# Hybrid encoder layer: first head pair's bias and cached k and v loaded behind the first norm, FFN block order, one more low part by DMA

## Chip, cores, metric

One core of a Trainium2 chip runs the whole layer in one launch. The metric is the device time of one execution in microseconds. TensorE (PE) does the matrix products, ScalarE (ACT) activations and copies, VectorE (DVE) and GpSimd (POOL) elementwise work, SyncE (SP) issues most of the transfers; POOL issues those that add into a tile.

## The reference

One inference step of one encoder layer for 512 new prompt frames and 64 frames of a running stream, 576 tokens of width 1024:

```python
h = layer_norm(ALPHA * x + 0.5 * swiglu_ffn(x, w_gu1, w_down1), g1, b1)
z = h @ w_in     # mLSTM q,k,v,o,i,f | attention q,k,v | two branch gates
# attention: 16 heads of 64, frames in chunks of 64, each sees its own and 8 chunks before;
# the stream's 64 frames see 256 cached k and v as well
s = einsum('bhqd,bhkd->bhqk', q, kk) + bias
o = einsum('bhqk,bhkd->bqhd', softmax(s), vv)
mix = (sigmoid(g_ml) * mlstm(...) @ w_ml + sigmoid(g_att) * o @ w_att) @ w_out
h = layer_norm(ALPHA * h + mix, g2, b2)
y = layer_norm(ALPHA * h + 0.5 * swiglu_ffn(h, w_gu2, w_down2), g3, b3)
```

with `swiglu_ffn(x) = (silu(gate) * up) @ w_down`, 2816 hidden columns. The outputs are `y`, the new mLSTM state, and the new k and v.

## The kernel before

**Products.** Every fp32 operand is split into a high part rounded to fp32r and a low part, the rest; a product is three matmuls, high by high, high by low and low by high (`mm`, L128). Weights come in blocks of 128x1024: SP loads `wr` (L208), ACT rounds it to `wh` (`act`, L142), and the low part `wl` comes in one of two ways. Either DVE subtracts (`tt`, L145). Or, for the keys in the set `ADDED`, ACT writes the negated high part into `wl` and POOL issues a second transfer of the same block that adds into it (`add_lo`, L180 to L182). `pump` (L193ff) keeps two raw and up to four split blocks ahead of the products.

**Units.** Most gate and up blocks of both FFNs, and 14 pairs of column blocks of `w_in`, go in units of seven products on sums and differences instead of eight products (`GateUp`, `Columns`). `Combos` makes the sums of the activations (`add`, DVE) and splits them (`make`, ACT, with the low part by POOL's adding DMA, into tiles `tx`, of which there are `NX`). `prep` splits a unit's weights: "a" (rows as loaded), "s" (sums into `ws` and `wt`), "t" and "u" (these sums), "b" (half a block, `ah` and `al`). `run` works through the units: first `begin` with the "a" part, then sums s2, s1, s3.

**Stages.** FFN 1 from 0 to about 395 us, the first norm and the first blocks of `w_in` (v, k, q of the first attention pair, and the mLSTM gates) to 440, column units to 520, attention with its eight pairs of heads to 790, gates and projections, the mLSTM, the output product with the second norm from 1160 to 1204, FFN 2 to the end with the last norm.

**Order.** PE's order is written out by the program: the class `Order` holds a heap of steps with due times (`later`) and takes them as the counted time of the matmuls passes. The other engines' orders come from a scheduler that follows PE's order, with priorities (`hot`, `high_priority`) and explicit successions (`issue_after`). Each engine then runs its list in order, so an instruction that waits holds up all behind it.

**Attention, per pair j of heads.** `att_qkv` (L1090ff) loads the bias `G` (two tiles of 128x512, `bias`, L1095 to L1105; POOL masks a corner of each, L1102), the cached values `vp` (L1111) and the cached keys `kp` (L1112). POOL splits `vp` into `vc` (L152 and L145), and `dup` splits keys into `kh` and `kl` for each head e of the pair and copies them to the other half of the partitions: for the new keys `kf` POOL and ACT write `kh`, DVE subtracts and copies `kl` (L1151); for the cached keys POOL does all. `att_core` computes `score(e, i)`, four blocks for each head, with softmax, transposes (`turn`) and split (`pth`, `ptl`), then `values(e)`; after the first head's scores comes `score_s`, the stream's 64 queries on cached and new keys. The due times of the steps count from the pair's start; the loads of pair 0 are issued there too, since the tiles of this stage's pool come free only at the end of the stage before.

Of the kernel before, what the change touches and what calls it, by code (L numbers as in the profile page):

```python
# [81 lines left out]
def tile_layer(ctx: ExitStack, tc: tile.TileContext, ins, outs):  # L82
# [71 lines left out]
    def pround(out, in_):  # L154
# [9 lines left out]
    NX = 10  # L164
# [4 lines left out]
        | {("ap", j) for j in range(KT)} | {("gu2", 1, 1), ("gu2", 2, 0)}  # L169
# [10 lines left out]
    def add_lo(lo, hi, src):  # L180
        act(lo, f(hi), scale=-1.0)
        POOL.dma_start(lo, src, accum_op=ALU.add)  # L182
# [10 lines left out]
    def pump(limit=2):  # L193
        while True:
# [16 lines left out]
            if c < wst["stop"] and c < wst["taken"] + limit and wst["used"] < NWB:  # L211
# [3 lines left out]
                if plan[c][0] == "if":  # L215

                    r3 = raw[:, :n].rearrange("p (k c) -> p k c", c=64)
                    h3 = hi.rearrange("p (k c) -> p k c", c=P)
                    act(h3[:, :, 0:64], r3)
                    tt(h3[:, :, 64:128], r3, f(h3[:, :, 0:64]), ALU.subtract)  # L220
                    parts[c] = (hi, None)
                else:
                    lo = wpool.tile([P, 1024], F32R, tag="wl", name=nm("wl"), bufs=NWB)
                    step = n if plan[c][0] not in PIECES else 512
                    for a in range(0, n, step):
                        act(hi[:, a:a + step], raw[:, a:a + step])
                        if plan[c][0] in ADDED:
                            add_lo(lo, hi, plan[c][1])
                            continue
                        before = wst.pop("behind", None)  # L230
                        with tc.issue_after(before.ins) if before is not None else nullcontext():
                            tt(lo[:, a:a + step], raw[:, a:a + step], f(hi[:, a:a + step]), ALU.subtract)
                    parts[c] = (hi, lo)
# [419 lines left out]
    class Combos:  # L653


        def __init__(self, xs, raw, sums):
            self.xs, self.raw, self.n, self.sums = xs, raw, 0, sums
            self.b = {}

        def tile(self):  # L660
            self.n += 1
            return slot(F32R, self.pool, "tx", bufs=NX) if self.n <= NX else slot(F32R)

# [10 lines left out]
        def make(self, middle):  # L674
# [3 lines left out]
            for n, (ka, kb) in ((1, ("t2", "t4")), (0, ("t1", "t3"))):  # L678
                for i in range(4):

                    t, hi, lo = self.sums[2 * i + n], self.tile(), self.tile()
                    with tc.issue_after(after.ins) if after is not None else nullcontext():
                        last = ACT.activation(hi, t, AF.Copy)
                        add_lo(lo, hi, t)
# [9 lines left out]
    class Units:  # L694
# [78 lines left out]
        def run(self, tail):  # L773
            cur = ahead = None
            for j in self.js + [None]:
# [13 lines left out]
                if j == self.js[0]:  # L789

# [107 lines left out]
    def ffn(xs, n, gi, raw, final=None, prev=None):  # L898
        hh = {}
        with tc.tile_pool(name=nm("hr"), bufs=FT, side="right", reuse_waits="tile") as hr, \  # L900
# [11 lines left out]
            def up_cb(j):  # L912
                return lambda hf, ps: tt(hs(hh[j], hf), hs(hh[j], hf), ps, ALU.mult)
# [29 lines left out]
            with wstack, tc.tile_pool(name=nm("st"), bufs=1, side="right", reuse_waits="tile") as un.tp, \  # L943
# [24 lines left out]
                after = un.prep(j0, "u")  # L968
                with tc.issue_after(after.ins):
                    un.prep(j0, "b")  # L970
# [120 lines left out]
    def att_qkv(j):  # L1091
        ap_ = apool[0]
        st = {}
        def bias():
            G = st["G"] = ap_.tile([P, 2, 512], F32, tag="G", name=nm("G"))  # L1095
# [3 lines left out]
            @hot(0 if j else 300)  # L1099
# [4 lines left out]
            later(4000 if j else 0, mask)  # L1104

        if j == 0:
            bias()
        vc = ap_.tile([P, 7, 2, P], F32R, tag="vc", name=nm("vc"), bufs=2)
        vp = ap_.tile([P, 2, P], F32, tag="vp", name=nm("vp"))
        kp = ap_.tile([P, NPAST], F32, tag="kp", name=nm("kp"))  # L1110
        SP.dma_start(vp, ins["vpast"][:, :, j * P:(j + 1) * P])  # L1111
        SP.dma_start(kp, ins["kpastT"][:, j, :])  # L1112
# [68 lines left out]
    def att_core(j, st):  # L1181
# [27 lines left out]
        def score(e, i):  # L1209
# [6 lines left out]
            ttr(sc[:, :w], ps[:, :w], G[:, e, 512 - w:512], mx[:, 0:1])  # L1216
# [26 lines left out]
        def score_s():  # L1243
            sc, mx = tiles()
            for e in range(2):
# [6 lines left out]
                ttr(sc[r, :320], ps[0:64, :320], G[0:64, e, 128:448], mx[r, 0:1])  # L1252
# [42 lines left out]
    combos = Combos(H, ln1.d, [slot(F32, stp, "st", bufs=8) for _ in range(8)])  # L1295
# [24 lines left out]
    ln1.close()  # L1320
    with tc.tile_pool(name="cx", bufs=1, side="right", reuse_waits="tile") as cx:
# [22 lines left out]
        after = un.prep(0, "u")  # L1344
        with tc.issue_after(after.ins):
            un.prep(0, "b")
# [479 lines left out]
```

## Time and profile before

| | |
|---|---|
| median of 3 runs | 1598.27 us (1597.28, 1598.27, 1598.95) |
| the profiled execution | 1598.74 us, its span 1597.0 us |
| PE busy | 1570.4 us, 98% |
| DVE, ACT, POOL busy | 1066.0, 885.2, 187.1 us |
| mean granted clock | 0.996 |
| moved by DMA | 202.88 MB, mean 127 GB/s |

A row of a timeline has its start, its duration, the engine, the line, the operation, output and inputs by the program's names, shape, and count; in brackets stands how long the engine had been idle before it and what ended that. A row with a count over 1 is a run of such instructions, and its duration is of them all together. A row of waits has the total, the number and the longest in microseconds. A window row has, for a stretch, each engine's busy time and instructions, then the granted TensorE clock, the DMA engines' share and the rate.

### The profile page before, as it was taken

The numbers are of one execution on the slowest core, as the hardware profiler recorded it, in microseconds if no ns is written. First come the engines' busy times: TensorE is split into PE (matmuls) and PEld (weight loads), VectorE is DVE, ScalarE is ACT, GpSimd is POOL, SyncE is SP. The second block draws the span as 40 slices with busy tenths as digits, with TensorE's granted clock in tenths as the row PEclk, the third lists the DMA queues.
The fourth block names the chain that finished last, engine by engine and source line by source line (L and its number), as shares of the span: only waits on it lengthen the run. The fifth ranks groups of instructions, "written<-read, shape, count | busy, mean of one in ns | idle before, by whom it ended". The sixth has DMA issues, their size and how long they took to land. (4 is left out here: it accounts for less than half of the span.)

```text
span 1597.0 us, 29481 instructions
## 1 busy us (share of the span) xinstructions
PE 1570.4 (98%) x11767; PEld 1548.2 (97%) x11767; DVE 1066.0 (67%) x2126; ACT 885.2 (55%) x1627; POOL 187.1 (12%) x350
## 2 busy tenths in 40 slices
PE   9999999999999899999999999999999999999998
PEld 8999999999999799999999999999999999999997
DVE  7777777627766657667613677755677787786636
ACT  7444455324855667777745876664456445454223
POOL 2000000000300433432111111101111000000000
PEclk9999999999999999999999999999999999999999
DMA  9232322225743666665788555543554222213333
GB/s 253 106 106 80 106 80 73 83 87 167 184 138 122 170 144 148 161 148 131 202 201 203 139 133 116 126 116 117 161 130 100 80 106 82 105 53 98 111 93 123
DMA packets 72113, 202.88 MB, mean 127 GB/s; under 512 B 7976, under 2 KB 17832, under 8 KB 71976
## 3 DMA queue, kind: packets, MB, share of 16 engines
q1 hardware_dynamic: 58584, 159.31, 30.7%
q0 software_dynamic: 12816, 41.16, 15.4%
q8 instruction: 92, 1.51, 0.4%
q10 hardware_dynamic: 576, 0.52, 0.1%
q14 instruction: 45, 0.37, 0.1%
HBM read 177.57 MB, written 16.32 MB: 121 GB/s over the span
## 5 line engine op out<-in xcount | busy, mean ns | idle before, releaser
L128 PE MATMUL mm<-s,wh 128*128 128x288 f32 (+2 forms) x3606 | 738.1, 298 | 1.5 <-ACT wh L142 0.9
L128 PEld LDWEIGHTS mm<-s,wh 128*128 128x128 f32 x3606 | 579.6, 189 | 5.5 <-ACT wh L142 1.1
L128 PE MATMUL mm<-s,wl 128*128 128x288 f32 (+2 forms) x1787 | 529.3, 296 | 1.1 <-DVE wl L145 1.1
L128 PEld LDWEIGHTS mm<-s,wl 128*128 128x128 f32 x1787 | 337.9, 189 | 1.7 <-DVE wl L145 1.7
L142 ACT ACTIVATE wh<-wr 128x1024 fp32r<-128x1024 f32 (+2 forms) x148 | 149.2, 1010 | 245.8 <-PE mm L128 225.3
L145 DVE TENSOR_TENSOR wl<-wr,wh 128x1024 fp32r<-128x1024 f32 (+2 forms) x87 | 100.1, 1155 | 101.1 <-ACT wh L142 101.1
L128 PE MATMUL mm<-h,wh 128*128 128x256 f32 (+1 forms) x672 | 134.7, 294 | 0.0
L128 PEld LDWEIGHTS mm<-h,wh 128*128 128x128 f32 x672 | 107.6, 188 | 0.2
L128 PE MATMUL mm<-tx,wh 128*128 128x288 f32 x522 | 107.0, 296 | 0.0
L128 PE MATMUL mm<-h,wl 128*128 128x256 f32 (+1 forms) x336 | 98.7, 294 | 0.0
L145 DVE TENSOR_TENSOR wl<-wt,wh 128x1024 fp32r<-128x1024 f32 x46 | 56.4, 1226 | 55.1 <-ACT wh L717 55.1
L717 ACT ACTIVATE wh<-wt 128x1024 fp32r<-128x1024 f32 x46 | 48.8, 1060 | 74.0 <-DVE wt L145 73.0
L450 POOL TENSOR_TENSOR rs<-var,mhalf 128x2 f32<-128x2 f32 (+1 forms) x6 | 5.2, 866 | 720.6 <-DVE var L148 720.6
L128 PEld LDWEIGHTS mm<-tx,wh 128*128 128x128 f32 x522 | 83.7, 188 | 0.0
L128 PE MATMUL mm<-tx,wl 128*128 128x288 f32 x261 | 77.0, 295 | 0.0
L182 POOL DMA_DIRECT2D wl<-in_w_in x50 | 44.0, 881 | 262.0 <-ACT wl L142 220.0
L128 PE MATMUL mm<-tx,ah 128*128 128x288 f32 x344 | 70.4, 297 | 0.0
L145 DVE TENSOR_TENSOR wl<-wu,wh 128x1024 fp32r<-128x1024 f32 x46 | 56.3, 1224 | 21.1 <-ACT wh L717 21.1
L142 ACT ACTIVATE h<-h 128x288 f32<-128x288 f32 x78 | 34.2, 438 | 63.8 <-DVE h L145 63.7
L717 ACT ACTIVATE wh<-wu 128x1024 fp32r<-128x1024 f32 x46 | 48.7, 1059 | 34.6 <-PE mm L128 33.9
L145 DVE TENSOR_TENSOR wl<-ws,wh 128x1024 fp32r<-128x1024 f32 x46 | 56.1, 1220 | 11.6 <-ACT wh L717 11.6
L142 ACT ACTIVATE wl<-wh 128x1024 fp32r<-128x1024 f32 x60 | 63.4, 1056 | 0.6
(342 smaller groups left out, 3485.0 us busy)
## 6 DMA issues: line engine op xcount, KB each, us to landing
wu<-in_w_gu SPq DMA_DIRECT2D x78, 512.0 KB, 4.4
wr<-in_w_in SPq DMA_DIRECT2D x58, 512.0 KB, 4.0
wl<-in_w_in POOLq DMA_DIRECT2D x50, 512.0 KB, 5.8
wr<-in_w_dn SPq DMA_DIRECT2D x40, 512.0 KB, 3.6
wr<-in_w_dn SPq DMA_DIRECT2D x20, 384.0 KB, 3.1
wu<-in_w_in SPq DMA_DIRECT2D x14, 512.0 KB, 4.8
G<-in_rbias SPq DMA_DIRECT2D x16, 256.0 KB, 2.9
wr<-in_w_ap SPq DMA_DIRECT2D x8, 512.0 KB, 4.7
```

The lines of the kernel that those rows point to most:

```text
L128: PE.matmul(out, lhsT, rhs, start=start, stop=stop, **kw)
L142: ACT.activation(out, in_, func, **kw)
L145: return (eng or DVE).tensor_tensor(out, a, b, op=op)
L182: POOL.dma_start(lo, src, accum_op=ALU.add)
L450: return y, POOL.tensor_tensor(y, v, mhalf[:, :n], op=ALU.pow)
L717: self.last = ACT.activation(hi, src, AF.Copy)
```

## The change

- **First attention pair.** The bias tiles, `vp` and `kp` of pair 0 are no longer loaded at the start of the attention stage. They go into tiles of the general slots (`past0`, `G0`), with the four loads written right behind the sums of the first norm, after `ln1.close()`; POOL's two masks follow the last adding DMA of `make` (`combos.added`). `G` becomes a list of two tiles. The other pairs' loads keep their text, and since pair 0 has none of its own there, the scheduler issues pair 1's earlier; in POOL's order the masks of pair 1 come to stand on either side of pair 0's last `kl` copy, where pair 0's own masks stood near the front.
- **tx tiles.** The units of `w_in` get 11 of them instead of 10 (`NX_IN`).
- **Second pair's first weight block sooner.** In the first round of `run`, for FFN 1, FFN 2 and the column units, "a" of the next unit is split ahead of "u" and "b" of the first; these two moved from before `run` into it.
- **FFN 1.** The multiplication by `up` of block 0 is set behind the low part of block (1,1) on DVE (`wst["lo"]`).
- **FFN 2.** The block (2,1) of gate and up joins `ADDED`: its low part by ACT's negated copy and POOL's adding DMA instead of DVE's subtraction.

PE's list of matmuls and their order are the same.

```diff
--- before.py
+++ after.py
@@ -161,12 +161,12 @@
     WARM = 8
     LAST = {1: 6, 2: 6}
     CL = {1: 2, 2: 3}
-    NX = 10
+    NX, NX_IN = 10, 11
     NH0, NH1 = 1, 6
     PIECES = {("in", 48), ("in", 40), ("in", 32)}
 
     ADDED = {("in", c + j) for c in (32, 40, 48) for j in range(2, KT)} | {("in", c) for c in (*range(32), *range(56, 72))} \
-        | {("ap", j) for j in range(KT)} | {("gu2", 1, 1), ("gu2", 2, 0)}
+        | {("ap", j) for j in range(KT)} | {("gu2", 1, 1), ("gu2", 2, 0), ("gu2", 2, 1)}
 
     EARLY = [("gu2", 0, 0), ("gu2", 0, 1), ("gu2", 1, 0)]
     EARLY1 = [("in", 16), ("in", 17)]
@@ -179,7 +179,7 @@
 
     def add_lo(lo, hi, src):
         act(lo, f(hi), scale=-1.0)
-        POOL.dma_start(lo, src, accum_op=ALU.add)
+        return POOL.dma_start(lo, src, accum_op=ALU.add)
 
     def early(pool, key, group):
         c = [k for k, _ in plan].index(key)
@@ -229,7 +229,7 @@
                             continue
                         before = wst.pop("behind", None)
                         with tc.issue_after(before.ins) if before is not None else nullcontext():
-                            tt(lo[:, a:a + step], raw[:, a:a + step], f(hi[:, a:a + step]), ALU.subtract)
+                            wst["lo"] = tt(lo[:, a:a + step], raw[:, a:a + step], f(hi[:, a:a + step]), ALU.subtract)
                     parts[c] = (hi, lo)
                 wst["used"] += 1
                 wst["conv"] += 1
@@ -653,13 +653,13 @@
     class Combos:
 
 
-        def __init__(self, xs, raw, sums):
-            self.xs, self.raw, self.n, self.sums = xs, raw, 0, sums
+        def __init__(self, xs, raw, sums, nx=NX):
+            self.xs, self.raw, self.n, self.sums, self.nx = xs, raw, 0, sums, nx
             self.b = {}
 
         def tile(self):
             self.n += 1
-            return slot(F32R, self.pool, "tx", bufs=NX) if self.n <= NX else slot(F32R)
+            return slot(F32R, self.pool, "tx", bufs=self.nx) if self.n <= self.nx else slot(F32R)
 
         def add(self, i):
             r1, r2 = self.raw[4 + i], self.raw[i]
@@ -681,7 +681,7 @@
                     t, hi, lo = self.sums[2 * i + n], self.tile(), self.tile()
                     with tc.issue_after(after.ins) if after is not None else nullcontext():
                         last = ACT.activation(hi, t, AF.Copy)
-                        add_lo(lo, hi, t)
+                        self.added = add_lo(lo, hi, t)
                     d = self.b.setdefault(i, {})
                     d[ka], d[kb] = (hi[:, a], lo[:, a]), (hi[:, b], lo[:, b])
                 if n:
@@ -787,6 +787,10 @@
                 with tc.high_priority(offset=90 if j == self.js[0] else 0):
                     self.prep(j + 1, "a")
                 if j == self.js[0]:
+                    with tc.issue_after(self.lo.ins):
+                        after = self.prep(j, "u")
+                    with tc.issue_after(after.ins):
+                        self.prep(j, "b")
 
                     ahead = self.begin(j + 1, "aux")
                 with tc.issue_after(self.lo.ins):
@@ -910,7 +914,10 @@
                 return cb
 
             def up_cb(j):
-                return lambda hf, ps: tt(hs(hh[j], hf), hs(hh[j], hf), ps, ALU.mult)
+                def cb(hf, ps):
+                    with tc.issue_after(wst["lo"].ins) if prev is None and j == 0 else nullcontext():
+                        tt(hs(hh[j], hf), hs(hh[j], hf), ps, ALU.mult)
+                return cb
 
             def key(j, e):
                 return [((f"gu{n}", j, e), KT)]
@@ -965,9 +972,6 @@
                         with tc.issue_after(combos.last.ins):
                             un.prep(j0, "s")
                         un.prep(j0, "t")
-                after = un.prep(j0, "u")
-                with tc.issue_after(after.ins):
-                    un.prep(j0, "b")
                 un.load(j0 + 2)
 
                 def tail():
@@ -1092,24 +1096,28 @@
         ap_ = apool[0]
         st = {}
         def bias():
-            G = st["G"] = ap_.tile([P, 2, 512], F32, tag="G", name=nm("G"))
+            G = ap_.tile([P, 2, 512], F32, tag="G", name=nm("G"))
+            st["G"] = [G[:, e, :] for e in range(2)]
             for e in range(2):
                 SP.dma_start(G[:, e, :], ins["rbias"][2 * j + e])
 
-            @hot(0 if j else 300)
             def mask():
                 for e in range(2):
                     POOL.memset(G[0:64, e, 448:512], NEG)
 
-            later(4000 if j else 0, mask)
-
+            later(4000, mask)
+
+        vc = ap_.tile([P, 7, 2, P], F32R, tag="vc", name=nm("vc"), bufs=2)
         if j == 0:
-            bias()
-        vc = ap_.tile([P, 7, 2, P], F32R, tag="vc", name=nm("vc"), bufs=2)
-        vp = ap_.tile([P, 2, P], F32, tag="vp", name=nm("vp"))
-        kp = ap_.tile([P, NPAST], F32, tag="kp", name=nm("kp"))
-        SP.dma_start(vp, ins["vpast"][:, :, j * P:(j + 1) * P])
-        SP.dma_start(kp, ins["kpastT"][:, j, :])
+            st["G"], vp, kp = G0, vp0, kp0
+            with tc.issue_after(combos.added.ins):
+                for e in range(2):
+                    POOL.memset(G0[e][0:64, 448:512], NEG)
+        else:
+            vp = ap_.tile([P, 2, P], F32, tag="vp", name=nm("vp"))
+            kp = ap_.tile([P, NPAST], F32, tag="kp", name=nm("kp"))
+            SP.dma_start(vp, ins["vpast"][:, :, j * P:(j + 1) * P])
+            SP.dma_start(kp, ins["kpastT"][:, j, :])
         vp4 = vp.rearrange("p b (e c) -> p b e c", c=64)
         for b in range(2):
             pround(vc[:, 5 + b, :, 0:64], vp4[:, b])
@@ -1213,7 +1221,7 @@
             mm(ps[:, :w], q, kh[:, e, :w], True, False)
             mm(ps[:, :w], q, kl[:, e, :w], False, True)
             sc, mx = tiles()
-            ttr(sc[:, :w], ps[:, :w], G[:, e, 512 - w:512], mx[:, 0:1])
+            ttr(sc[:, :w], ps[:, :w], G[e][:, 512 - w:512], mx[:, 0:1])
             softmax(sc, mx, w, lambda: turn(e, i, sc))
 
         def turn(e, i, sc):
@@ -1249,7 +1257,7 @@
                     mm(ps[0:64, s0:s0 + n], q, kh[:, e, kk:kk + n], True, False)
                     mm(ps[0:64, s0:s0 + n], q, kl[:, e, kk:kk + n], False, True)
                 r = slice(64 * e, 64 * e + 64)
-                ttr(sc[r, :320], ps[0:64, :320], G[0:64, e, 128:448], mx[r, 0:1])
+                ttr(sc[r, :320], ps[0:64, :320], G[e][0:64, 128:448], mx[r, 0:1])
             softmax(sc, mx, 320, lambda: turn_s(sc))
 
         def turn_s(sc):
@@ -1292,7 +1300,7 @@
     stp = pstack.enter_context(tc.tile_pool(name="st", bufs=1, side="right", reuse_waits="tile"))
     e1 = pstack.enter_context(tc.tile_pool(name="early1", bufs=1, side="right", reuse_waits="tile"))
     cw = pstack.enter_context(tc.tile_pool(name="cw", bufs=1, side="right", reuse_waits="tile"))
-    combos = Combos(H, ln1.d, [slot(F32, stp, "st", bufs=8) for _ in range(8)])
+    combos = Combos(H, ln1.d, [slot(F32, stp, "st", bufs=8) for _ in range(8)], NX_IN)
 
     VD, OD = [away("vd") for _ in range(KT)], [away("od") for _ in range(KT)]
 
@@ -1318,6 +1326,14 @@
     for i in range(4):
         combos.last = combos.add(i)
     ln1.close()
+
+    past0 = slot(F32)
+    vp0, kp0 = past0[:, 0:NPAST].rearrange("p (b c) -> p b c", c=P), past0[:, NPAST:2 * NPAST]
+    G0 = [slot(F32)[:, 0:512] for _ in range(2)]
+    SP.dma_start(vp0, ins["vpast"][:, :, 0:P])
+    SP.dma_start(kp0, ins["kpastT"][:, 0, :])
+    for e in range(2):
+        SP.dma_start(G0[e], ins["rbias"][e])
     with tc.tile_pool(name="cx", bufs=1, side="right", reuse_waits="tile") as cx:
         combos.pool = cx
 
@@ -1341,9 +1357,6 @@
                 with tc.issue_after(combos.last.ins):
                     un.prep(0, "s")
                 un.prep(0, "t")
-        after = un.prep(0, "u")
-        with tc.issue_after(after.ins):
-            un.prep(0, "b")
         un.load(2)
 
         def tail():
```

## Prediction

> **What bounds the kernel now.** I read the page's busy shares first, then the waits of TensorE, then the timeline of each engine around the waits that stand where the diff edits, then windows for the granted clock.
>
> ```profile
> span 1597.0 us, 29481 instructions
> PE 1570.4 (98%) x11767; PEld 1548.2 (97%) x11767; DVE 1066.0 (67%) x2126; ACT 885.2 (55%) x1627; POOL 187.1 (12%) x350
> ```
>
> TensorE is busy for all but 1597.0 - 1570.4 = 26.6 us, and the change leaves its matmuls and their order alone. So only two things can move: the 26.6 us in which it waits, and the time its matmuls take when the clock is halved. Here is who ended its waits (total, times, longest):
>
> ```profile
> PE aux L128 <- POOL kl L152: 4.8, 2, 3.3
> ...
> PE mm L128 <- DVE s L145: 1.2, 1, 1.2
> PE mm L128 <- DVE wl L145: 1.1, 2, 0.9
> ...
> PE aux L128 <- DVE wl L145: 0.7, 1, 0.7
> PE aux L128 <- POOL kh L152: 0.7, 1, 0.7
> ```
>
> The edits touch three places in this list. The two waits for POOL's `kl` and the one for its `kh` (5.5 us) lie in the sample scores of the first attention pair. The two for DVE's `wl` (0.9 and 0.7) lie in the first FFN. The one for DVE's `s` (1.2) lies at the start of the second FFN. Other waits are out of reach.
>
> **Attention, first pair: the bias and the cached k and v.** TensorE's timeline, with the wait before each row in brackets:
>
> ```profile
> 526.97 0.33 PE L128 MATMUL aux<-kl,qs 128*128 128x128 f32 x1 [0.41 <-DVE kl L1151]
> ...
> 533.51 0.33 PE L128 MATMUL aux<-kh,qs 128*64 128x256 f32 x1 [0.66 <-POOL kh L152]
> 535.38 0.33 PE L128 MATMUL aux<-kl,qs 128*64 128x256 f32 x1 [1.54 <-POOL kl L152]
> ...
> 539.46 0.47 PE L128 MATMUL aux<-kl,qs 128*64 128x256 f32 x1 [3.27 <-POOL kl L152]
> ...
> 539.91 0.47 PE L138 MATMUL aux<-ident,sc 128*128 128x128 f32 x1
> ...
> 551.48 0.50 PE L128 MATMUL aux<-ptl,vc 128*128 128x512 f32 x1 [2.04 <-DVE mx L152]
> ```
>
> And POOL's, which is what they wait for:
>
> ```profile
> 522.39 0.87 POOL L182 DMA_DIRECT2D wl<-in_w_in  x1 [87.03 <-ACT wl L142]
> 523.17 1.62 POOL L152 TENSOR_SCALAR kh<-kf 64x576 fp32r<-64x576 f32 x2
> 527.30 0.14 POOL L1102 MEMSET G<- 64x64 f32 x1 [2.51 <-DMA G<-in_rbias]
> 530.14 0.14 POOL L1102 MEMSET G<- 64x64 f32 x1 [2.69 <-DMA G<-in_rbias]
> 530.97 0.64 POOL L152 TENSOR_SCALAR vc<-vp 128x128 fp32r<-128x128 f32 x2 [0.68 <-DMA vp<-in_vpast]
> ...
> 539.01 0.40 POOL L152 TENSOR_SCALAR kl<-kl 64x256 fp32r<-64x256 f32 x1
> ```
>
> POOL stands still three times, 2.51 + 2.69 + 0.68 = 5.88 us, for loads that were issued only when the stage began; its last `kl` then ends at 539.4 and TensorE's at 539.46 can go. The change issues these four loads behind the first norm and masks the bias there (POOL has next to nothing to do until its 87.03 us wait ends), so the three stops go. Windows (columns: us, busy and instructions by engine, granted clock, DMA share, GB/s):
>
> ```profile
> 420.00:424.00 4.00, 4.00 (x28) 4.00 (x28) 4.00 (x12) 3.33 (x7) 0.87 (x1) 1.00 0.01 1
> 523.20:539.45 16.25, 10.33 (x72) 9.33 (x70) 10.22 (x31) 9.52 (x20) 9.60 (x22) 0.92 0.70 199
> 536.60:540.00 3.40, 0.54 (x4) 0.54 (x5) 0.00 (x0) 0.00 (x0) 2.64 (x7) 0.52 0.50 92
> 540.00:543.40 3.40, 3.40 (x15) 3.36 (x15) 1.44 (x10) 2.03 (x7) 0.00 (x0) 0.50 0.65 140
> 983.80:987.20 3.40, 2.18 (x15) 1.80 (x16) 2.90 (x7) 3.40 (x12) 0.77 (x5) 1.00 0.36 98
> 1035.00:1038.40 3.40, 2.17 (x14) 1.60 (x14) 2.78 (x7) 3.34 (x11) 0.50 (x4) 1.00 0.01 2
> 1038.40:1041.80 3.40, 3.40 (x18) 3.40 (x18) 3.37 (x8) 3.35 (x6) 0.26 (x2) 0.51 0.39 113
> ```
>
> From 523.20 to 539.45 POOL works 9.60 us (second row). In the new order the weight block's DMA issue among these (0.87, as at 522.39) and one memset (0.14) come behind the last `kl`; the second pair's first memset stays in front of it. That leaves 8.6 us, and a POOL that starts at 523.2 and never stops ends its last `kl` at 531.8. TensorE asks for the first sample `kh` at 533.51 - 0.66 = 532.85 and, with the waits out, for the last `kl` about 1.1 us later: 2.1 us to spare. So 0.66 + 1.54 + 3.27 = 5.47 us goes.
>
> Two small terms come with it. The few matmuls in the 536.60 window ran at clock 0.52; at full clock their 0.54 us is 0.27, a gain of 0.27. Against that, POOL now splits the cached v before the pair's `kh`, and DVE puts all four `qs` products and a `vc` subtraction ahead of `kl`'s copy, so the first score's wait (0.41) grows. It can't grow by more than the v work put in front (0.64 at 530.97 and a subtraction of its size) and not by less than nothing; I take 0.5 of 0 to 1.5. Net: 5.47 + 0.27 - 0.5 = 5.2 us.
>
> What is late next is the first `values`, which in the profile waits 2.04 us for DVE at 551.48. From 539.91 to 551.48 are 11.57 us; TensorE worked 11.57 - 2.04 = 9.53 of them, and 3.40 of those at clock 0.50 (540.00 window), which is 1.7 us of loss. In the changed kernel the long stop is gone, the clock should hold, and TensorE arrives after 7.8 us. But `values` waits for a chain of score, softmax, transpose and split on DVE and ACT, which shortens only where it waited for the slow matmuls. If none of it shortens the gain is 0; if all, 1.7; most of the slow stretch is scores and transposes that feed this chain, so I take 1.3. `values` then still waits 11.57 - 1.3 - 7.8 = 2.5 us, and the gain up to it is 5.2 + 1.3 = 6.5 us.
>
> Then the clock. The grid in the trace is stretches of 3.41 us, and the clock of one follows from how busy the one before was. The 1035.00 window has 2.17 us of TensorE in it (1.23 idle) and the next is at 0.51; the 983.80 window has 2.18 and its next stretch was at full clock. So the edge lies near 1.2 us of idle time in one stretch. A wait of 2.5 us, however it falls on the grid, puts at least 1.25 into one. I expect one stretch at half clock behind it, 1.7 us by the 540.00 row: 6.5 - 1.7 = 4.8.
>
> The Trainium skill, page "TensorE: Matmul & The Clock Gate", section "Why this matters for your kernels", holds otherwise: only gaps of over about 3 us, a whole idle window, bring the half clock back. By it the 2.5 us costs nothing more, and the 1035.00 row, half clock after 1.23 us, disagrees with it.
>
> Covers of this part. The four new loads go out at the end of the norm, when the DMA is at 0.01 of its share (420.00 row), ahead of two stores that nobody on the chip reads; taken as 0, at worst some tenths at the next weight block. POOL's two memsets wait there for the last of the `tx` sums, with nothing urgent behind. An 11th `tx` tile replaces a slot: 0. The second pair's v, k and bias loads are issued earlier, and its bias now has POOL waiting on it:
>
> ```profile
> 521.53 0.99 SPq L1097 DMA_DIRECT2D G<-in_rbias  x2
> ...
> G<-in_rbias SPq DMA_DIRECT2D x4, 256.0 KB, 5.7
> ```
>
> In the changed order these issues take the first pair's place, some 2 us later because a store must land first, so about 524; by the 5.7 us the bias is there at 530, before POOL gets to its memset at about 531.4. Taken as 0.
>
> **First FFN.** Here `wl` of (1,1) goes ahead of the gate multiplication, and the second pair's block `a` is split before `u`.
>
> ```profile
> 25.41 0.42 DVE L145 TENSOR_TENSOR h<-h,mm 128x256 f32<-128x256 f32 x1 [2.52 <-ACT h L909]
> 25.75 0.45 DVE L148 SCALAR_TENSOR_TENSOR h<-h,s 128x288 f32<-128x288 f32 x1
> 26.12 1.22 DVE L145 TENSOR_TENSOR wl<-wr,wh 128x1024 fp32r<-128x1024 f32 x1
> ...
> 35.68 1.23 DVE L145 TENSOR_TENSOR wl<-ws,wh 128x1024 fp32r<-128x1024 f32 x1 [0.48 <-ACT wh L717]
> 37.20 1.23 DVE L145 TENSOR_TENSOR wl<-wu,wh 128x1024 fp32r<-128x1024 f32 x1 [0.29 <-ACT wh L717]
> ...
> 38.48 0.40 PE L128 MATMUL aux<-s,wl 128*128 128x288 f32 x1 [0.73 <-DVE wl L145]
> ```
>
> DVE idled 2.52 us for ACT; in that time now fall the last sum (0.45) and `wl` (1.22), which ends near 24.6 and not at 27.34: the 0.9 us wait goes. Further on `a` is the split at 37.20, which TensorE gets at 38.48. In the slot of 35.68 it ends 1.52 us sooner, and TensorE reaches its matmul 0.9 + about 0.25 sooner, so it still waits some 0.4 there. The gain of the stage is what the later point moves: 1.5 us. `u`, now after `a`, is used a whole product later. Bounds: 0.9 (the rest is taken back by the next late piece, a low part that POOL's DMA brings) to 1.6.
>
> **Start of the second FFN.** The low part of (2,1) goes from DVE to a negated copy on ACT and a DMA that POOL issues.
>
> ```profile
> 1184.48 1.05 ACT L142 ACTIVATE wl<-wh 128x1024 fp32r<-128x1024 f32 x1
> ...
> 1187.72 0.42 ACT L142 ACTIVATE s<-s 128x256 fp32r<-128x256 f32 x1
> ...
> 1189.38 0.40 PE L128 MATMUL mm<-s,eh 128*128 128x256 f32 x2
> ...
> 1200.13 1.21 DVE L145 TENSOR_TENSOR wl<-wr,wh 128x1024 fp32r<-128x1024 f32 x1
> ...
> 1204.88 0.42 PE L128 MATMUL mm<-s,eh 128*128 128x320 f32 x1 [1.20 <-DVE s L145]
> ```
>
> DVE's 1.21 us lay inside the norm's second half, whose next piece TensorE waits 1.20 us for: 1.1 goes (0.9 to 1.2). The copy (1.05, by the 1184.48 row) falls on ACT ahead of the norm's first steps. The first high part ended at 1188.14 and would end at 1189.2, just before TensorE's 1189.38; its low part follows and may cost 0.25 (0 to 1.0). Net 0.85 (-0.1 to 1.2). The DMA issue falls on an idle POOL. `a` before `u` here: no wait of TensorE stands there, 0.
>
> **The sum.** 1.5 + 4.8 + 0.85 = 7.2 us less. The profiled execution took 1598.74 us (span 1597.0 and 1.7 around it); the median of the runs is 1598.27, 0.47 below. From the median: 1591.1 us. Runs of before lie 1.67 us apart, as much as one stretch at half clock; so 0.2%, 3.2 us, is about what can be told from no change.
>
> **Rivals.**
> (A) The clock holds after the 2.5 us wait, as it did behind 983.80 and as the page named above has it: 1.5 + 6.5 + 0.85 = 8.9, 1589.4 us. Against it: 1035.00.
> (B) The forecast.
> (C) A new wait takes part of the place of the old. Second-pair loads now stand in POOL's order ahead of the first pair's last `kl`. If they land 5 us later than reckoned (rows of bias loads show POOL stopped 2.51 and 2.69 us at a time when several share the queues), TensorE waits some 3 us again, 7.2 - 3 = 4.2 at most and with a longer first-score wait 3.5: 1594 to 1595 us. For it: DMA share 0.70 over 523.20 to 539.45. Against: the loads it would run with are fewer.
> (D) Slower: the same mechanism at full size. POOL's memset of the second pair's bias holds the first pair's last `kl`, needed at about 534. The 7.2 us is used up when the memset ends at 541, and over 0.2% slower begins at 544.5, so a bias landing 20 us after its issue at 524, against 5.7: 1601.5 us and above.
> (E) The change doesn't do what it says: POOL's own work, not the loads, holds `kl`. Then the 5.5 us stays and 1.5 + 0.85 = 2.35 remains: 1595.9. Against it: the three stops with the DMA named, and 8.6 us of work in a 16.25 us window.
>
> **How the numbers follow.** B 0.58, A 0.18, C 0.12, E and lesser gains 0.08, D 0.04. The likeliest is B: 1591.1. A with the better ends of the small terms gives 1588; C's end is 1595. Those hold 8 in 10: 1588.0 to 1595.0. The threshold for faster is 1595.1: A, B and nearly all of C, 0.87; the same 0.08 (E and the rest); slower 0.05.
>
> **What would show it.** In the changed trace POOL's rows from 523 to 532 without stops, the sample scores' three waits gone and the transpose of 539.91 at about 533 (1.5 us earlier from the first FFN, 5.2 from here); a wait of 2.5 us before the first `values` and a stretch near 0.5 after it; `wl` of (1,1) ending before 25; no or short wait at 1204.88's matmul. Wrong: a memset of the bias on POOL that still waits for its DMA inside 523 to 535, a wait of `values` above 3.5, or a new wait near 425 or 1189.

## Result, and the profile after

The changed kernel takes 1588.62 us (median of five) where the kernel before, on the same chip, takes 1597.86: the ratio is 0.9941, 95% interval 0.9924 to 0.9958, so 9.4 us less (6.7 to 12.1); the medians differ by 9.2. A second comparison gave 1589.19 against 1596.91, 0.9943 (0.9929 to 0.9956). The forecast was 1591.1 from 1598.27, 7.2 us less.

One of the five, the first profiled execution of the changed kernel, ran at a granted clock of 0.556 throughout (2533.3 us), so the ratio leaves it out and its waits tell nothing; all rows "of the changed kernel" below come from a second execution of the same program at clock 0.996, 1589.82 us with a span of 1588.0. First its busy shares and TensorE's waits (total, times, longest):

```profile
span 1588.0 us, 29486 instructions
...
PE 1569.3 (99%) x11767; PEld 1549.3 (98%) x11767; DVE 1066.2 (67%) x2125; ACT 884.7 (56%) x1628; POOL 189.0 (12%) x351
```

```profile
PE aux L128 <- DVE kl L1159: 2.8, 1, 2.8
...
PE aux L128 <- DVE mx L152: 2.1, 1, 2.1
...
PE aux L128 <- DVE wl L145: 0.5, 1, 0.5
...
PE mm L128 <- DVE s L145: 0.2, 1, 0.2
```

TensorE's idle time is 18.7 us instead of 26.6. The waits for POOL's `kh` and `kl` are out of the list, the 1.2 us for `s` is 0.2, the 0.9 us for `wl` in the first FFN is gone. But the wait for `kl` on DVE, 0.4 before, is now the longest of all. TensorE's timeline at the four places:

```profile
37.17 0.40 PE L128 MATMUL aux<-s,wl 128*128 128x288 f32 x1 [0.49 <-DVE wl L145]
...
527.31 0.33 PE L128 MATMUL aux<-kl,qs 128*128 128x128 f32 x1 [2.81 <-DVE kl L1159]
...
535.27 0.33 PE L138 MATMUL aux<-ident,sc 128*128 128x128 f32 x1
...
545.21 0.50 PE L128 MATMUL aux<-ptl,vc 128*128 128x512 f32 x1 [2.06 <-DVE mx L152]
...
1195.97 0.42 PE L128 MATMUL mm<-s,eh 128*128 128x320 f32 x1 [0.15 <-DVE s L145]
```

Set beside the same matmuls of before, these starts show what each stage gave in this pair of executions: 38.48 to 37.17 is 1.3 us from the first FFN; at the first score's `kl` TensorE asks at 524.50 instead of 526.56, 2.1 us; at the first `values` 551.48 to 545.21, 6.3 us, so 4.2 from the start of the attention. Behind it stands a stretch at half clock, and the next common wait (753.39 and 748.66) is only 4.7 us sooner. At 1203.68 and 1195.82, the ends of the work ahead of the last wait, it is 7.9 again: there the kernel before had its own half-clock stretch at 1038 and longer waits in the mLSTM, which the change doesn't touch. The end is 9.0 sooner, 1.1 of it from the second norm. Single executions thus differ by 3 us in places that have nothing to do with the change, and the comparison over several runs is the one to trust.

Two parts of these differences need care. The start of the program varies: one and the same matmul of 128x256 took 0.41 us at 9.12 in this trace and 0.28 at 8.13 in that of before, so TensorE was 1 us behind here, for reasons that lie ahead of the first edit. The nine traces whose first FFN is the changed one have the matmul of 37.17 between 35.78 and 38.42, with 36.52 in the middle, so the first FFN gives 0.1 to 2.7 us against the one trace of before, in the middle 2.0. And of the 2.1 us at 524.50, 0.66 came between the first FFN and the attention: a wait for ACT's `wh`, 0.88 us at 401.59 before, is 0.23 here. It is 0.19 in the trace of the kernel before with only the early loads as well, whose first FFN and norm are as before, so it isn't shown to be the change's.

Why the first score waits is in POOL's and DVE's timelines of the changed kernel:

```profile
520.90 1.15 POOL L152 TENSOR_SCALAR vc<-s 128x128 fp32r<-128x128 f32 x2
521.68 1.21 POOL L145 TENSOR_TENSOR vc<-s,vc 128x128 fp32r<-128x128 f32 x2
522.63 0.90 POOL L152 TENSOR_SCALAR kh<-kf 64x576 fp32r<-64x576 f32 x1
...
531.58 0.40 POOL L152 TENSOR_SCALAR kl<-kl 64x256 fp32r<-64x256 f32 x1
```

```profile
520.96 3.88 DVE L148 SCALAR_TENSOR_TENSOR qs<-qf,qs 64x256 fp32r<-64x256 f32 x4 [3.68 <-ACT qs L142]
524.94 1.09 DVE L145 TENSOR_TENSOR kl<-kf,kh 64x576 fp32r<-64x576 f32 x1
525.96 0.68 DVE L145 TENSOR_TENSOR vc<-aux,vc 128x512 fp32r<-128x512 f32 x1
526.66 0.59 DVE L1159 CAST kl<-kl 64x576 fp32r<-64x576 f32 x1
```

The same place in DVE's timeline of before:

```profile
523.02 1.24 DVE L148 SCALAR_TENSOR_TENSOR qs<-qf,qs 64x256 fp32r<-64x256 f32 x2 [3.68 <-ACT qs L142]
524.36 1.03 DVE L145 TENSOR_TENSOR kl<-kf,kh 64x576 fp32r<-64x576 f32 x1
525.42 1.00 DVE L148 SCALAR_TENSOR_TENSOR qs<-qf,qs 64x320 fp32r<-64x320 f32 x2
526.46 0.45 DVE L1151 CAST kl<-kl 64x576 fp32r<-64x576 f32 x1
```

POOL now runs without a stop and ends its last `kl` at 531.98. Before, it also began beside DVE (523.17 and 523.02), but stopped for the first bias tile after 1.62 us; now it goes on, and both are slow: the four `qs` products take 3.88 us where before they took 1.24 and 1.00, and POOL's rounding of the cached v takes 1.15 where it took 0.64. The copy of `kl` ends at 527.25, and TensorE, there since 524.50, can go.

### The profile page after: what moved, and what is told of

It is laid out like the page before. It is cut to its first block, busy times and chain, and to the rows that moved or that the text cites. A ratio compares the mean times of both kernels' runs of the same rounds, so it can differ in the third digit from the quotient of the medians.

```text
span 2533.3 us, 29486 instructions
## 1 busy us (share of the span) xinstructions
PE 2525.0 (100%) x11767; PEld 2314.7 (91%) x11767; DVE 1088.6 (43%) x2125; ACT 903.5 (36%) x1628; POOL 189.0 (7%) x351
## 4 chain that ended last, share of the span: by engine, by line
PE 99%; DMA 0%; DVE 0%; ACT 0%; issue 0%; DVEq 0%
PE mm L128 85%; PE aux L128 12%; PE aux L138 3%; DMA w<-in_w_gu 0%; DVE s L148 0%; PE mm L138 0%; DVE vl L145 0%; DVEq L1818 0%; ACT vh L142 0%; ACT wh L438 0%; ACT s L427 0%
## 5 line engine op out<-in xcount | busy, mean ns | idle before, releaser
L128 PE MATMUL mm<-s,wh 128*128 128x288 f32 (+2 forms) x3593 | 1112.3, 409 | 0.5 <-ACT s L427 0.5
L128 PEld LDWEIGHTS mm<-s,wh 128*128 128x128 f32 x3593 | 780.8, 235 | 61.6 <-issue 3.0
L128 PE MATMUL mm<-s,wl 128*128 128x288 f32 (+2 forms) x1774 | 722.6, 407 | 0.0
L128 PEld LDWEIGHTS mm<-s,wl 128*128 128x128 f32 x1774 | 418.7, 236 | 26.2
L128 PE MATMUL mm<-h,wh 128*128 128x256 f32 (+1 forms) x672 | 207.0, 408 | 0.0
L128 PE MATMUL mm<-hb,wh 128*128 128x256 f32 (+1 forms) x280 | 85.9, 406 | 0.0
L128 PE MATMUL mm<-hc,wh 128*128 128x256 f32 (+1 forms) x280 | 85.8, 405 | 0.0
L128 PEld LDWEIGHTS mm<-h,wl 128*128 128x128 f32 x336 | 78.1, 233 | 4.8
L128 PE MATMUL mm<-os,wh 128*128 128x256 f32 (+1 forms) x256 | 79.0, 409 | 0.0
L128 PE MATMUL mm<-H,wh 128*128 128x256 f32 (+1 forms) x256 | 78.6, 412 | 0.0
```

Of the source, the lines that this page charges most:

```text
L128: PE.matmul(out, lhsT, rhs, start=start, stop=stop, **kw)
```

## The experiments

**The early loads alone, both ways.** Undone in the changed kernel (with 10 `tx` tiles again), and put alone into the kernel before (with 11):

```diff
-            st["G"], vp, kp = G0, vp0, kp0
+            bias()
+            vp = ap_.tile(...); kp = ap_.tile(...)
+            SP.dma_start(vp, ...); SP.dma_start(kp, ...)
```

The changed kernel itself, for its second profile:

> The changed kernel itself, for a profile at full clock. Both theories: some 9 us under the kernel before (1588 to 1590 where that has 1597 to 1598). Theory 1 (half clock behind the wait of the first values): a wait of about 2.5 us there and a stretch of 3.4 us near 0.5 after it; gain of the attention stage 4.8 us. Theory 2 (the clock holds there): the same wait, clock 1.00 after it, gain of the stage 6.5 us. In both the sample scores wait for nothing, and the second FFN's wait of 1.20 us at the norm's second half is under 0.3.

> The changed kernel with the first pair's bias and cached k and v loaded at the start of the attention stage again (and 10 tx tiles), all else as changed. If the loads carry the gain as forecast, this gives back 4.8 us (theory 1) or 6.5 us (theory 2) and is 1.5 + 0.85 = 2.35 us under the kernel before. If POOL's own work held the scores, it is as fast as the changed kernel.

> The kernel before with only the early loads (and 11 tx tiles). Theory 1: 4.8 us under the kernel before. Theory 2: 6.5 us. If the parts don't add up, this and the run without the early loads together give another sum than the changed kernel's 9 us. Its trace also shows the wait of the first values and the clock behind it.

Without the early loads: 1593.60 us, ratio to before 0.9979 (0.9970 to 0.9988), 4.4 us over the changed kernel's 1589.19 by the medians and 5.7 by the ratios; in its trace POOL's `kl` is back as the longest wait:

```profile
PE aux L128 <- POOL kl L152: 4.8, 2, 3.3
```

With them alone: 1593.13 us, 0.9975 (0.9966 to 0.9984), 3.8 to 4.0 us under before. So the loads are what held POOL, they carry about half of the gain, and 4.8 us was about right as a sum. They also bring the first score's longer wait: it is 0.40 us without them, and 2.68 to 2.84 in the six traces that have them and POOL's and DVE's work as the changed kernel. The other edits together give 3.4 us (1.9 to 4.8) by the first of these ratios.

In the same two traces the first `values` waits again, 2.03 and 2.05 us, and in neither does the clock fall behind it; behind the changed kernel's 2.06 it did. So on the clock neither theory held as stated; more on it below.

**The low part of (2,1) on DVE again.**

```diff
-        | {...} | {("gu2", 1, 1), ("gu2", 2, 0), ("gu2", 2, 1)}
+        | {...} | {("gu2", 1, 1), ("gu2", 2, 0)}
```

> The changed kernel with the low part of (2,1) in the second FFN by DVE's subtraction again. Forecast: 0.85 us slower than the changed kernel (0 to 1.2), with the wait of 1.20 us at the norm's second half back and no wait near the first matmul of the second FFN. Rival: the ACT copy costs as much at that first matmul as it saves later, then the two are within 0.3 us.

```profile
1194.41 0.41 PE L128 MATMUL mm<-s,eh 128*128 128x320 f32 x1 [1.19 <-DVE s L145]
```

The wait is back, 1.19 against 0.15, and neither trace has a wait at the second FFN's first matmul: the move is worth 1.04 us there, and the ACT copy costs TensorE nothing. The time, 1589.63 us and 0.9961 (0.9948 to 0.9974), is too coarse for this: the intervals overlap.

**"u" ahead of "a" again.**

```diff
+                after = un.prep(j0, "u")
+                with tc.issue_after(after.ins):
+                    un.prep(j0, "b")
                 un.load(j0 + 2)
```

(and out of `run`; likewise for the column units)

> The changed kernel with "u" and "b" of the first unit split before "a" of the second again, in all three units stages; the multiplication by up stays behind the low part. Forecast: the wait at the first FFN's second unit, 0.49 us in the changed kernel, becomes about 0.25 + 0.73 + the 0.9 by which TensorE comes sooner = 1.9; so some 1.4 us slower than the changed kernel. Rival: the split order matters nowhere, since the first unit's low part alone was late: the same time.

```profile
37.20 0.53 PE L128 MATMUL aux<-s,wh 128*128 128x288 f32 x2 [1.23 <-ACT wh L717]
38.46 0.40 PE L128 MATMUL aux<-s,wl 128*128 128x288 f32 x1 [0.73 <-DVE wl L145]
```

1.23 + 0.73 = 1.96 us of waits in place of 0.49: TensorE comes to these matmuls sooner by the earlier `wl`, and stands longer. The earlier low part without the earlier "a" gives back all of it in this trace (38.46 against 38.48 in the kernel before). The earlier "a" without the earlier low part was not run. The time: 1590.06 us, 0.9961 (0.9947 to 0.9975), 0.9 over the changed kernel by the medians, its intervals overlapping too.

**Is the first score late by contention or by order?** In the changed kernel two things differ from before: POOL stays busy beside DVE, and DVE has all four `qs` products ahead of `kl`. One run keeps POOL as busy and gets DVE's old order back (the cached v split last); another takes POOL's work away from that place (the cached k and v are split in the column units' stage, into three general slots that the sample steps read; it ran from 510.44 to 518.18). DVE's order at the first score is the same in both.

```diff
-        for b in range(2):          # in att_qkv, shortened: pair 0's part
-            pround(vc[:, 5 + b, ...]); tt(vc[:, 5 + b, ...], ..., POOL)
+        later(6600, past_v)         # the same loop, v split last
```

```diff
+    vs0, kh0, kl0 = ...             # shortened; split early: three slots
         combos.make(middle)
+        with tc.issue_after(combos.added.ins):
+            split_past()            # the same 12 POOL instructions on vp0, kp0
```

> The changed kernel with pair 0's cached v split by POOL after the cached keys; DVE's order is then the one of before (kl and its copy ahead of the second half of qs), and POOL is as busy as in the changed kernel. Theory P: qs products still near 0.9 us each and kl over 1.0, first score's wait 0.7 to 1.5 because fewer of them stand ahead of kl; 1 to 2 us faster than the changed kernel. Theory O: qs products near 0.55 each, wait about 0.4, 2 to 3 us faster.

> The changed kernel, and POOL splits the cached k and v of pair 0 in the column units' stage, where it idles, into three general slots that the sample steps read; at the attention's start POOL has only the splits of the new k and of pair 1's v left. Theory P (POOL and DVE slow each other when both run on SBUF tiles; that is why four qs products took 3.88 us where two and two took 1.24 + 1.00): the qs products of DVE that run without POOL beside them take 0.5 to 0.6 us each, those beside the first kh about 0.6 to 0.9; the first score's wait falls from 2.81 to under 0.8 and no half clock follows; 2 to 4 us faster than the changed kernel. Theory O (only DVE's order, all four qs products ahead of kl, makes the first score late): DVE's order here has kl before the second half of qs, so the wait falls too, but a qs product still takes 0.97 us.

DVE's rows, first of the run with v split last, then of the one with the early split:

```profile
519.70 1.79 DVE L148 SCALAR_TENSOR_TENSOR qs<-qf,qs 64x256 fp32r<-64x256 f32 x2 [3.68 <-ACT qs L142]
...
522.39 1.78 DVE L148 SCALAR_TENSOR_TENSOR qs<-qf,qs 64x320 fp32r<-64x320 f32 x2
```

```profile
520.23 1.29 DVE L148 SCALAR_TENSOR_TENSOR qs<-qf,qs 64x256 fp32r<-64x256 f32 x2 [3.68 <-ACT qs L142]
...
522.68 1.00 DVE L148 SCALAR_TENSOR_TENSOR qs<-qf,qs 64x320 fp32r<-64x320 f32 x2
```

Same order, same instructions: 1.78 us with POOL working beside them, 1.00 with POOL idle (its `kh` was done at 522.05). That is the contention. Not every instruction pays: in the first of these runs `kl`, which also reads two tiles in SBUF, took 0.76 us at 521.59 with POOL working beside it, while POOL's subtraction at 521.84 took 1.11, against 0.74 for the one that ran with DVE idle (516.95 in the run with the early split). The order has a share as well. The first score's wait in the two:

```profile
524.81 0.33 PE L128 MATMUL aux<-kl,qs 128*128 128x128 f32 x1 [1.57 <-DVE kl L1164]
```

```profile
524.23 0.33 PE L128 MATMUL aux<-kl,qs 128*128 128x128 f32 x1 [0.46 <-DVE kl L1160]
```

From 2.81 to 1.57 is the order, at the durations that contention gives, and from 1.57 to 0.46 the contention. In these waits theory P holds, with O beside it (1.57 lies just above P's 0.7 to 1.5, 0.46 under its 0.8). The times don't resolve it: v split last 1587.39 us, 0.9942 (0.9928 to 0.9955), early split 1586.15 us, 0.9933 (0.9921 to 0.9946). By the medians they lie 1.8 and 3.0 us under the changed kernel, by the ratios 0.2 and 1.6, and the intervals overlap with its 0.9929 to 0.9956.

The Trainium skill has this rule: page "SBUF — State Buffer", section "Who interferes with whom", says that a VectorE instruction with two inputs in SBUF contends with a GpSimd instruction that reads SBUF, and that the port pair they share is an exclusive lock. Pair 0's `qs` products read `qf` and `qs`, both in SBUF, and the runs agree that they suffer; over two products they show a stretch to 1.8 times. This rule bore on the change, and the forecast didn't weigh it.

**The wait before the first values.** The forecast had it as the length of a chain on DVE and ACT. Three tries: the `values` step 2.6 us later in TensorE's order, and a higher priority on DVE for the `ptl` that it waits for, in the changed kernel and in the one with the early split.

```diff
+    LATE = 2600
...
-                later(2720, lambda: values(e))
+                later(2720 + (LATE if j == 0 and e == 0 else 0), lambda: values(e))
```

```diff
+            with tc.high_priority(offset=60) if j == 0 and e == 0 and i == 3 else nullcontext():
                 tt(tl[:, 0:i + 1, i, :], v4, f(th[:, 0:i + 1, i, :]), ALU.subtract)
```

> The changed kernel with pair 0's first values due 2.6 us later in TensorE's order, so that other products run while DVE and ACT finish the chain to ptl. The wait of 2.06 us before values should go, with the half clock that followed it in one execution: 2.0 us faster than the changed kernel, 2 to 3.7 with the clock. Rival: TensorE has nothing ready to put there and the wait appears at another step: no change.

> The changed kernel with only the priority of that ptl. If the wait before the first values (2.06 us, and a half clock after it in one of the traces) is DVE's order and not the length of the chain, it falls under 0.5 here as well: 1.5 to 2 us faster than the changed kernel. If it is the chain, as the prediction had it, the wait stays at about 2.

> The kernel with the cached k and v split early, and pair 0's last ptl of the first head given a higher priority on DVE, so that it stands ahead of pair 1's kl (1.16 us), a softmax scaling (0.82) and kl's copy (0.57), which came first while TensorE waited 2.52 us for ptl. Expected: that wait falls to under 0.5, since pth ends 536.88 and ptl 3.4 us later for these three; some 2 us faster than with the early split alone, 4 to 5 under the changed kernel. Rival: the displaced kl and scaling make pair 1's scores or the next transposes wait as long: no change.

Values later: 1588.19 us, 0.9944 (0.9931 to 0.9956); the 2.06 us became 0.85, 0.16 and 0.67 at the next steps, 1.7 together. Priority alone: 1589.25 us, 0.9955 (0.9942 to 0.9967). Priority with the early split: 1585.63 us, 0.9928 (0.9914 to 0.9941), no clear difference to the early split. In the last two `values` no longer waits, and the next transposes do; first the priority alone, then with the early split:

```profile
546.43 0.52 PE L138 MATMUL aux<-ident,sc 128*128 128x128 f32 x3 [1.98 <-DVE psl L145]
```

```profile
542.35 0.52 PE L138 MATMUL aux<-ident,sc 128*128 128x128 f32 x3 [2.50 <-DVE psl L145]
```

My expectation of about 2 us fell in all three, since the wait went to later steps. With the priority `values` itself waits for nothing, so it wasn't held by the length of its own chain. DVE's rows in the changed kernel, up to `values` at 545.21, show what stood ahead of its `ptl`, pair 1's `kl` and its copy (the profile puts the wait down to the short `mx` that ends just behind the `ptl`):

```profile
542.05 0.73 DVE L145 TENSOR_TENSOR kl<-s,kh 64x576 fp32r<-64x576 f32 x1
...
543.61 0.84 DVE L1159 CAST kl<-kl 64x576 fp32r<-64x576 f32 x1
544.46 0.69 DVE L145 TENSOR_TENSOR ptl<-aux,pth 128x512 fp32r<-128x512 f32 x1
545.07 0.14 DVE L152 TENSOR_SCALAR mx<-mx 128x1 f32<-128x1 f32 x1
```

The trace of before has the same order, `kl` at 548.33 and `ptl` at 550.74. DVE is behind by 2 to 2.5 us at this place, and whatever TensorE asks for next waits for it. That the backlog is DVE's work, not its order, was tried last: pair 1's `kl`, ahead of that `psl` (the low part of the stream's scores), moved to POOL. DVE's rows with the early split and the priority, which show it there:

```profile
538.62 0.94 DVE L145 TENSOR_TENSOR kl<-s,kh 64x576 fp32r<-64x576 f32 x1
...
540.66 1.17 DVE L145 TENSOR_TENSOR kl<-s,kh 64x576 fp32r<-64x576 f32 x1
...
541.94 0.26 DVE L145 TENSOR_TENSOR psl<-aux,psh 64x128 fp32r<-64x128 f32 x1
```

```diff
+                if j == 1:
+                    tt(kl[r, e, cc], src[r], f(kh[r, e, cc]), ALU.subtract, POOL)
+                    pround(kl[o, e, cc], f(kl[r, e, cc]))
+                else: ...                # on DVE as before
```

> The kernel with the early split and the ptl priority, and pair 1's kl (two subtractions and two copies, 0.94 + 1.17 + 0.64 and one more copy on DVE) made by POOL instead, which has time until pair 1's first score at 552. Theory: the 2.50 us wait at the transposes is the backlog of DVE, 2.75 us of which is this kl, ahead of the second psl; without it the wait falls to about 0.5 and the kernel is 2 us faster than with the two edits. Rival: POOL's work beside DVE's slows DVE's operations with two SBUF inputs, and POOL's own cached keys come later; the wait shrinks by under 1 us or the time stays.

```profile
539.74 0.28 DVE L145 TENSOR_TENSOR psl<-aux,psh 64x128 fp32r<-64x128 f32 x1
```

```profile
540.17 0.52 PE L138 MATMUL aux<-ident,sc 128*128 128x128 f32 x3 [0.29 <-DVE psl L145]
```

The wait went from 2.50 to 0.29, and the traces agree in size: the next common wait ends at 741.13, with the two edits alone at 743.26. The time is 1583.22 us, 0.9916 (0.9900 to 0.9932), 2.4 us under the kernel with the two edits by the medians; the intervals overlap. This is the fastest version run here, 14 us under the kernel before and 5 to 6 under the changed one by the medians. POOL beside DVE costs DVE little at this place (the `psl` above 0.28 against 0.26), though POOL's own subtraction takes 1.4 us.

## Why the prediction came out

**First FFN, 1.5 us.** 1.3 in this pair of traces and 2.0 in the middle of nine, above the forecast's upper end of 1.6; `wl` of (1,1) ran at 23.29, in the time in which DVE had idled, and a wait of 0.49 stayed at the second pair, 0.4 forecast. That mechanism is shown. The run with "u" first shows that the earlier low part alone isn't enough.

**Second norm, 0.85.** 1.04 in the wait; the 0.25 allowed for the first matmul wasn't paid.

**The loads, 5.47 us of waits.** All three are gone. That POOL's last `kl` ended at 531.98, where the sum said 531.8, is luck: POOL began 2.3 us sooner than before (520.90), and its work to this point took 11.1 us in place of 8.6. The slower work did no harm, since TensorE, itself late by the first score, came to this `kl` only at 535.07. Pair 1's bias on POOL held nothing: its memset ran at 531.35 without a stop, so the slower rival (D) had no ground, nor (E) with POOL's own work as the bound. (C) had the cause wrong, but the longer first-score wait that it names came.

**The first score, the step that failed.** I took 0.5 more wait, with 1.5 as the upper end; it was 2.40 more (2.81 against 0.41). The bound was built from POOL's v work in front of `kh`, at durations that POOL had while DVE hardly competed, and from DVE's instructions at the durations of a trace in which POOL was stopped for loads. Taking the stops away made the two engines run together, and what the stops had hidden was contention. The sign of the order on DVE was seen, its price not. By the two runs on the splits, 1.24 us of the wait is the order and 1.11 the contention.

**Values, 2.5 us of wait.** 2.06 in the changed kernel, 2.52 with the early split. From the transposes to `values` the changed kernel takes 545.21 - 535.27 = 9.94 us and not 11.57, so 1.63 was gained there, 1.3 forecast, and TensorE's part is 7.9, 7.8 forecast. The cause was only half right: DVE is late, as the forecast had it, but not by the chain of score, softmax, transpose and split. With the `ptl` given priority `values` waits for nothing, and with pair 1's `kl` off DVE the wait is gone, so what TensorE outran was the sum of DVE's work, pair 1's included.

**The clock, near in the number of stretches, wrong in place and in rule.** Forecast: one stretch after `values`, since the edge lay near 1.2 us of idle time; outside the mLSTM the traces put it near 1.8 (last section). In the changed kernel's trace there are two, one behind the first score and one behind `values`; but of the eight traces in which `values` waited 2.0 to 2.5 us (before, the changed kernel, the runs without and with only the loads, with the low part on DVE, "u" first, and the two on the splits), only the changed kernel's has a half clock behind that wait. Behind the first score's wait of 2.68 to 2.84 us it came in four of six traces. So the 1.7 us taken off for `values` should mostly have stayed in, as rival A had it, and the 1.9 us more of first score, with the clock behind that, took its place. These errors have opposite signs and cancel in good part, and that is luck: 4.8 forecast for the stage, 3.8 to 5.7 measured. The time of 1588.62 lies nearer to rival A's 1589.4 than to the 1591.1 forecast, though A didn't have the first score's wait either. Of the rest of the difference between 7.2 forecast and 9.4 measured, whose interval begins at 6.7, some 0.5 is the first FFN in the middle of the traces; more isn't resolved by these runs.

## What to carry to other kernels

When a wait is taken away, ask which engines it kept apart: durations from a trace in which POOL stood still are not those of one in which it runs beside a DVE instruction with two SBUF inputs. Work that is early by its data (a cache, a table) can be split early too, not only loaded, and an engine that idles for 85 us, as POOL did here, is the place for it. The wait that DVE's backlog caused moved when the order was changed, and went only when work left DVE: ask which of the two an edit does.

## What the runs showed of the hardware

The granted clock changes at the edges of stretches of 3.41 us. When windows of this length are laid so that the edges of a trace's half-clock stretches fall on them, the busy time of TensorE in one window nearly always tells the clock of the next. Two windows of the changed kernel, each ahead of a half-clock stretch (columns as in the prediction):

```profile
525.47:528.88 3.41, 1.57 (x13) 1.57 (x14) 3.25 (x8) 2.82 (x3) 3.23 (x6) 1.00 0.89 248
542.53:545.94 3.41, 1.35 (x9) 0.99 (x8) 3.35 (x7) 2.76 (x5) 3.01 (x6) 1.00 0.13 54
545.94:549.36 3.42, 3.42 (x17) 3.38 (x16) 2.87 (x8) 2.43 (x9) 2.34 (x3) 0.50 0.31 56
```

The kernel before with only the early loads, where the same wait of `values` left 1.65 us of busy time, and no half clock followed:

```profile
543.99:547.40 3.41, 1.65 (x14) 1.33 (x11) 3.38 (x7) 3.05 (x6) 3.01 (x6) 1.00 0.40 137
547.40:550.81 3.41, 3.12 (x22) 3.07 (x23) 3.28 (x11) 3.01 (x9) 3.10 (x5) 1.00 0.07 18
```

And the run with `values` later, whose first score waited 2.82 us as in the changed kernel, but across the edge of two stretches; both stayed above and the clock held:

```profile
521.09:524.50 3.41, 2.09 (x16) 1.94 (x15) 3.27 (x3) 3.34 (x6) 3.18 (x7) 1.00 0.92 187
524.51:527.92 3.41, 1.92 (x16) 1.92 (x17) 3.25 (x8) 2.47 (x3) 3.24 (x6) 1.00 0.89 246
527.92:531.33 3.41, 3.41 (x27) 3.33 (x26) 2.90 (x15) 2.50 (x9) 2.97 (x8) 1.00 0.54 168
```

Over the traces of all kernels, outside the start, the mLSTM and the last 20 us, and apart from stretches that were themselves at half clock, those with 1.57 us or less were followed by half clock and those with 1.65 or more by full: an edge a little under half of the stretch. So a wait of 2 us halves the clock when nearly all of it falls into one stretch, which changes from one execution to the next. Three things don't fit. In the tail of the kernel before, a stretch with 1.52 us was followed by full clock:

```profile
1588.03:1591.45 3.42, 1.52 (x14) 1.28 (x12) 3.33 (x6) 0.00 (x0) 0.70 (x1) 1.00 0.00 0
1591.45:1594.86 3.41, 0.00 (x0) 0.00 (x0) 2.21 (x4) 0.00 (x0) 0.00 (x0) 1.00 0.70 261
```

In the mLSTM a stretch with 2.20 us busy was followed by half clock in the kernel before and in the run with early split and ptl priority, and in five others with 2.20 to 2.23 us it wasn't; its matmuls are narrow, 130 columns on half of the rows. And in the run with the ptl priority alone a half-clock stretch full of work was followed by another. What is counted in place of busy time isn't settled.

The Trainium skill, page "TensorE: Matmul & The Clock Gate", section "Part 1: The HAM clock gate (the "warmup" mystery)", has the window of 3413 ns and that it runs freely, and the traces agree; that it takes a whole idle window, they don't, since 1.84 us idle in one (3.41 - 1.57) was enough here.
